# Hybrid recurrent block on one core: the first norm's token tiles transposed by products with a diagonal of their roots, norm weights as a scale of the operands, first units by column halves

## The chip, the core and the metric

The kernel runs on one core of a Trainium2 chip. The metric is the device time of one execution in microseconds (us); lower is better. The engines of the core are named as the profile names them: PE (TensorE, matrix products) with its weight loads PEld, DVE (VectorE), ACT (ScalarE), POOL (GpSimd) and SP (SyncE, which here only starts transfers). Data lie in SBUF, products land in PSUM banks.

## The reference

One layer over 528 tokens: 16 meta tokens ahead of 512 tokens of x, each of 1024 features. What the change touches is the first norm and the first columns of the product behind it.

```python
def rms_norm(x, g):
    y = x32 * lax.rsqrt(jnp.mean(x32 * x32, axis=-1, keepdims=True) + EPS)
    return (y * g.astype(jnp.float32)).astype(x.dtype)
...
    h = jnp.concatenate([meta, x], axis=1)
...
        xn = rms_norm(h, norm_mix_g[l])
        z = xn @ w_in[l]
        u_rnn, u_gate, q, k, v, g_ret, ga, gb = jnp.split(z, IN_SPLITS, axis=-1)

        xr = causal_dwconv(u_rnn, rnn_conv_w[l], rnn_conv_b[l])
        hr = rg_lru(xr, rg_a_w[l], rg_a_b[l], rg_x_w[l], rg_x_b[l], lru_lambda[l])
        o_a = hr * jax.nn.gelu(u_gate)
...
        mixed = (jax.nn.sigmoid(ga) * (o_a @ w_branch_rnn[l])
                 + jax.nn.sigmoid(gb) * (o_b @ w_branch_ret[l]))
        h = h + mixed @ w_out[l]
```

`u_rnn` has 1280 columns, ten blocks of 128; a gated linear recurrence runs on them (`rg_lru`, whose gates are two block-diagonal 128x128 products). Behind it come a retention branch with four heads, the mixture, a second norm, a convolved feed-forward part and a last norm. All are in f32, and the kernel keeps that accuracy.

## The kernel before, in words

**Operands in two parts.** Every f32 operand of a large product is split in two f16 parts: `split` (L90 to L92) writes the high part with ACT (L91: source times a scale, rounded to f16) and the rest with DVE (L92: source times scale minus high part). A product is then three f16 products, high by high, high by low and low by high (`project`, L370, and `project_half`, L383). The normed tokens lie transposed, feature on partition, in `xh` and `xl`: 8 feature blocks by 3 zeros and 528 tokens.

**Weights in units.** A unit is a block of weight columns. `unit_load` (L186) takes a raw f32 buffer out of a ring of two (`wraw`), starts its transfer, and gives back two steps that split the unit's two halves into `wt` tiles. The first ten blocks of `w_in` (the columns of `u_rnn`) are two units of 128 columns, one for each of blocks 0 and 1, and four units of 256 columns. Transfers are started on SP's queue in program order; `load` (L96) keeps them in that order. A transfer into a raw buffer starts when DVE has split what lay there.

**When steps are issued.** In the loops, `tick` takes the next split step of the queue unless the tiles from the unit in use up to that step's unit (two a unit) would be more than six; then it returns with nothing done. `get` issues what the next product needs. A step of unit u first starts the loads up to unit u+1.

**The prologue.** x comes in four token tiles of 128 tokens, two to a buffer `xin`. ACT squares and sums (L320), takes the root (L322), DVE inverts it (L324). `first_rows` (L398) multiplies the tile by its roots and by `gmix`, the norm weights broadcast to 128 partitions by a 512 KB transfer. `first_transpose` (L404) transposes its eight blocks on PE (L411), and `finish` splits them into `xh` and `xl`. The 16 meta tokens go another way: `xmeta` holds them as 128 rows of 128, a product with `same` (L442) sums their squares, and one with `pick` (L441) spreads the weights; then one transposition (L452). `keep_warm` (L424) is a number of products of zeros. `first_half(n)` (L388) multiplies block n of `u_rnn` with the first 267 columns, that is meta and tiles 0 and 1; `conv_product(n)` (L525) does the other half for n below 3, and whole blocks beyond. The order in the prologue, and in the whole kernel, is the order of the code: the engines run their instructions as written (`manual_schedule`, L429).

**The convolution loop** (L579 to L595) over n from 0 to 9: product n; at n of 0 the split of the gate weights "a" (`gw`); from n = 3 on, a tick and the gates of block n-3; then `conv_taps(n)`: ACT writes tap 3 with the bias (L537), DVE adds three taps (L539). For n below 2 a tick stands behind the taps. At n = 2 block 0 is split (`xs`, for the gates' product), then the gate weights "x", then block 1. The gates of block 0 run on PE between products 3 and 4 (L370 with `gw`), and their sigmoids on ACT (L556).

**Small vectors.** `v1`, `v2` hold convolution weights and biases row by row; after the last `first_half` three transpositions (L492 to L494) put them into PSUM as `ptv`, and DVE copies them out (L496 to L502: `vt1`, `vt2`, `gfT`, and `cwr`, the taps' factors).

`dec_meta`, a part of the decay table of the retention, is read from token chunk 0 of each head on (L718), and is loaded at L689.

## Time and profile before

| | |
|---|---|
| median of 3 runs | 1078.27 us (1078.19 to 1080.12) |
| profiled execution, its own time | 1080.82 us |
| its span | 1079.1 us |
| mean granted clock of PE | 0.998 |
| PE busy | 1059.0 us, 98% |
| DVE busy | 839.4 us, 78% |
| ACT busy | 568.2 us, 53% |
| POOL busy | 6.9 us, 1% |

A row of the timeline has the start in the span, the duration, the engine, the line, the operation, what it writes and reads, and shapes; "xN" is a run of N alike that stands as one row, its duration being from the first start to the last end. The brackets tell how long the engine had been idle, and what released it. In the chain of waits a row is start, duration, and what stood on the path that ended last. A row of the table of windows has the stretch and its length, then busy time and number of instructions for PE, PEld, DVE, ACT and POOL, the granted PE clock, the DMA engines' share and GB/s. DMA rows on SP are the issue alone; a reader's idle time shows the landing.

### The profile page before, as it was taken

What the parts mean: (1) busy time and instruction counts of PE and PEld (TensorE: products, weight loads), DVE (VectorE), ACT (ScalarE), POOL (GpSimd) and SP (SyncE); (2) the same over time, 40 slices, a digit from 0 to 9 for tenths busy, and PEclk for the clock granted to TensorE, in tenths of its full rate; (3) what the DMA queues carried; (4) which work ended last, traced back from release to release, by engine and by line L of the source; (5) the groups of instructions that cost most, each with busy time, mean ns of one, the idle gap of its engine ahead of it and who ended that gap; (6) DMA issues with size and microseconds to landing.
All of it is one profiled execution on the core that took longest, in us unless ns stands there. A gap on an engine that the chain in (4) does not pass through costs nothing.

```text
span 1079.1 us, 20969 instructions
## 1 busy us (share of the span) xinstructions
PE 1059.0 (98%) x9045; PEld 856.6 (79%) x9045; DVE 839.4 (78%) x1220; ACT 568.2 (53%) x847; POOL 6.9 (1%) x20
## 2 busy tenths in 40 slices
PE   8999999999999999999999999999999999999997
PEld 5888888875684858888888885588888888888885
DVE  5875699998786969888697785478767776888875
ACT  6568963534564747566454453364544454454442
POOL 2000000000000000000000000000000000000000
PEclk9999999999999999999999999999999999999999
DMA  6423243431211311433333355053232323113322
GB/s 209 143 92 104 79 138 118 157 119 40 75 45 50 108 64 65 125 91 118 104 103 118 118 199 173 2 196 115 81 118 80 118 79 118 40 60 121 115 79 79
DMA packets 105957, 112.02 MB, mean 104 GB/s; under 512 B 3470, under 2 KB 97396, under 8 KB 105864
## 3 DMA queue, kind: packets, MB, share of 16 engines
q1 hardware_dynamic: 105432, 110.27, 31.1%
q8 instruction: 71, 1.16, 0.4%
q10 hardware_dynamic: 144, 0.26, 0.1%
q14 instruction: 22, 0.18, 0.1%
q0 software_dynamic: 288, 0.14, 0.0%
HBM read 108.57 MB, written 2.10 MB: 103 GB/s over the span
## 4 chain that ended last, share of the span: by engine, by line
PE 71%; DVE 17%; ACT 8%; issue 2%; DMA 2%; SPq 0%; ACTq 0%; DVEq 0%
PE ps L370 33%; PE P L1247 9%; PE pa L775 7%; DVE wt L92 4%; PE ps L838 4%; PE pm L370 4%; PE ps L1119 3%; PE ps L383 3%; PE pe L775 3%; ACT wt L91 2%; PE pb L775 2%; PE ps L860 1%; DVE rnn L574 1%; DVE raw L231 1%; DMA raw<-in_w_out 1%
## 5 line engine op out<-in xcount | busy, mean ns | idle before, releaser
L370 PEld LDWEIGHTS <-wt 128*128 128x128 f16 x4224 | 410.5, 97 | 63.7 <-DVE t L666 1.4
L92 DVE SCALAR_TENSOR_TENSOR wt<-raw,wt 128x1024 f16<-128x1024 f32 (+2 forms) x270 | 296.2, 1110 | 71.7 <-ACT wt L91 69.8
L91 ACT ACTIVATE wt<-raw 128x1024 f16<-128x1024 f32 (+2 forms) x270 | 256.1, 964 | 161.3 <-PE ps L370 28.3
L775 PEld LDWEIGHTS <-wt 128*128 128x128 f16 x2016 | 195.0, 97 | 36.0 <-issue 8.8
L370 PE MATMUL ps<-x2h,wt 128*128 128x258 f16 x1440 | 218.8, 273 | 0.0
L370 PE MATMUL ps<-xh,wt 128*128 128x257 f16 (+2 forms) x1056 | 163.8, 275 | 1.1 <-DVE t L666 1.1
L370 PE MATMUL ps<-x2l,wt 128*128 128x258 f16 x720 | 137.7, 272 | 0.0
L1204 DVE SCALAR_TENSOR_TENSOR cv<-ps,vt,cv 128x512 f32<-128x512 f32 x96 | 71.9, 748 | 54.5 <-ACT cv L1202 53.2
L370 PE MATMUL ps<-xl,wt 128*128 128x257 f16 (+2 forms) x528 | 102.2, 275 | 0.0
L1247 PE MATMUL P<-wt,act 128*128 128x256 f16 x792 | 88.3, 273 | 0.0
L1247 PEld LDWEIGHTS <-act 128*128 128x128 f16 x792 | 77.5, 98 | 9.0
L838 PE MATMUL ps<-wt,xh 128*128 128x512 f16 x256 | 76.4, 379 | 1.2 <-DVE v L92 1.0
L775 PE MATMUL pa<-xs,wt 128*128 128x257 f16 x576 | 71.6, 273 | 4.8 <-ACT kept L780 4.5
L1202 ACT ACTIVATE cv<-ps,vt,vt 128x512 f32<-128x512 f32 x48 | 37.1, 774 | 56.8 <-PE ps L370 52.2
L370 PE MATMUL pm<-oa,wt 128*128 128x257 f16 x480 | 55.4, 274 | 0.0
L838 PEld LDWEIGHTS <-xh 128*128 128x128 f16 x256 | 24.8, 98 | 30.9 <-issue 2.9
L838 PE MATMUL ps<-wt,xl 128*128 128x512 f16 x128 | 48.5, 379 | 0.0
L775 PE MATMUL pa<-ob,wt 128*128 128x257 f16 x384 | 45.7, 274 | 0.6 <-ACT last L780 0.5
L1119 PE MATMUL ps<-wt,mx 128*128 128x512 f16 x192 | 44.8, 379 | 0.5 <-DVE mx L92 0.5
L231 DVE TENSOR_TENSOR raw<-raw 128x1024 f32<-128x1024 f32 x35 | 42.7, 1220 | 0.6
L1119 PEld LDWEIGHTS <-mx 128*128 128x128 f16 x192 | 17.4, 98 | 19.2 <-DVE mx L92 1.0
L860 PE MATMUL ps<-sc,v 128*128 128x257 f16 (+4 forms) x384 | 32.1, 236 | 0.0
(253 smaller groups left out, 1278.1 us busy)
## 6 DMA issues: line engine op xcount, KB each, us to landing
raw<-in_w_in SPq DMA_DIRECT2D x41, 1024.0 KB, 4.9
raw<-in_w_up SPq DMA_DIRECT2D x24, 1024.0 KB, 5.0
raw<-in_w_down SPq DMA_DIRECT2D x48, 256.0 KB, 3.6
raw<-in_w_branch_ret SPq DMA_DIRECT2D x16, 512.0 KB, 4.0
raw<-in_w_branch_rnn SPq DMA_DIRECT2D x8, 640.0 KB, 4.2
raw<-in_w_out SPq DMA_DIRECT2D x4, 1024.0 KB, 4.9
xin<-in_x SPq DMA_DIRECT2D x4, 512.0 KB, 6.6
h<-in_x SPq DMA_DIRECT2D x4, 512.0 KB, 4.9
```

Source lines behind the costliest of these rows:

```text
L91: nc.scalar.activation(hi, src, AF.Copy, scale=s)
L92: nc.vector.scalar_tensor_tensor(lo, src, s, hi, op0=ALU.mult, op1=ALU.subtract)
L231: nc.vector.tensor_tensor(pair, pair, rv[:, :, right].rearrange("p (h k) c -> p h k c", h=2), op=ALU.add)
L370: nc.tensor.matmul(ps[:, hf, :n], w(aw, k, col, P), src(ax, k, c0, n), start=k == 0 and (aw, ax) == (0, 0), stop=k == nk - 1 and aw == 1)
L383: nc.tensor.matmul(ps[:, hf, :n], w(aw, k, col, P), src(ax, k, c0, n), start=k == 0 and (aw, ax) == (0, 0), stop=k == KD - 1 and aw == 1)
L775: nc.tensor.matmul(ps[:, :257], ws[k // 4](wf, aw, k % 4), src(xf_, ax, k), start=first and k == 0 and (aw, ax) == (0, 0), stop=k == last_ ...
L838: nc.tensor.matmul(pb, xf(ax, k, XF + j0, nb), w(aw, k % 4, 0, 512), start=i == 0, stop=i == 23)
L860: nc.tensor.matmul(ps[:, hf, s0 - lo_i:257], vt[b][:, va, d * P:(d + 1) * P], st[SCP[b][0]][:, sa, o:o + hi_i - s0], start=i == 0, stop=i ...
L1119: nc.tensor.matmul(ps[:, n], mx[k][:, a, c0:c0 + P], wo[k // 2](aw, k % 2, n * 512, 512), start=j == 0, stop=j == 23)
L1202: nc.scalar.activation(vv_, ps[:, :, 2:258], AF.Identity, scale=vt2[:, 96 + ch:97 + ch], bias=b_ff[:, ch:ch + 1])
L1204: nc.vector.scalar_tensor_tensor(vv_, ps[:, :, j:j + 256], vt2[:, 48 * j + ch:48 * j + ch + 1], vv_, op0=ALU.mult, op1=ALU.add)
L1247: nc.tensor.matmul(pd[:, 256 * tt:256 * tt + 256], t[:, ax, c0 + tt * P:c0 + tt * P + P], w(wf, aw, i), start=q % 6 == 0 and tt == 0 and i ...
```

## The change

Each token tile was multiplied by its roots and the norm weights on DVE and then transposed. Now DVE makes a 128x128 diagonal of the tile's roots (`dg`), and PE multiplies each 128x128 block of the raw tile with that diagonal in f32; the product is the transposed block, already times the roots. The norm weight of a feature is now the weight of a partition, so it is applied as the scale operand when the product is split: `gs` holds eight columns of 128 weights, which PE transposes out of the 8x128 rows that `xmeta` already has. With one scale per block the split of a tile is eight ACT pieces and eight DVE pieces of 128x128 in place of two and two of 128x512. `gmix` and its transfer are gone. The transfer of the 8x128 weights moves from SP's queue to ACT's; that of `dec_meta` moves from the head of SP's queue into the chain of loads, behind a unit that is loaded much later.

The two units of 128 columns become one of 256, so that `u_rnn` is five units. The first two are loaded and split by column halves (`column_unit`): first the 128 columns of one block, then those of the other. Both are loaded in the prologue, so what was the third 256-column load there is gone. The products of zeros become 15, 4 and 6, from 18, 2, 5 and 6. The products of tiles 2 and 3 stand behind `first_half(1)` and behind `first_half(2)`; before, the transpositions stood behind `first_half(0)` and behind `first_half(1)`.

```diff
@@ -113,9 +113,7 @@
 
     o_ur, o_ug, o_q, o_k, o_v, o_gr, o_ga, o_gb = 0, 1280, 2560, 3584, 4608, 6656, 8704, 9728
     u_ur = []
-    for n in range(2):
-        u_ur.append((unit(8, P, [(0, 0, kmaj(w_in, 0, 8, o_ur + P * n, P))]), 0))
-    for i in range(1, 5):
+    for i in range(5):
         u = unit(8, 256, [(0, 0, kmaj(w_in, 0, 8, o_ur + 256 * i, 256))])
         u_ur += [(u, 0), (u, P)]
     u_ug = [unit(8, 256, [(0, 0, kmaj(w_in, 0, 8, o_ug + 256 * i, 256))]) for i in range(5)]
@@ -209,6 +207,30 @@
         wviews.append(lambda a, k, c0, m: tiles[k // hk][:, a, k % hk * ncol + c0:k % hk * ncol + c0 + m])
         return [step(i, c) for i in range(2) for c in range(cuts)]
 
+    def column_unit():
+        _, ncol, parts, _ = units[len(loaded)]
+        raw = wraw.tile([P, 2048], F32, name="raw")
+        rv = raw.rearrange("p (k c) -> p k c", c=ncol)
+        ap = parts[0][2]
+        tiles = []
+        def fetch(c):
+            load(rv[:, :, c * P:c * P + P], ap[:, :, c * P:c * P + P])
+        def step(i, c):
+            def run():
+                if c == 0:
+                    tiles.append(wsp.tile([P, 2, 1024], F16, name="wt"))
+                tv = [tiles[i][:, a].rearrange("p (k c) -> p k c", c=ncol)[:, :, c * P:c * P + P] for a in range(2)]
+                split(tv[0], tv[1], rv[:, 4 * i:4 * i + 4, c * P:c * P + P], SW)
+            return run
+        loaded.append(len(loaded))
+        wviews.append(lambda a, k, c0, m: tiles[k // 4][:, a, k % 4 * ncol + c0:k % 4 * ncol + c0 + m])
+        queue([step(i, c) for c in range(2) for i in range(2)])
+        return fetch
     def fast_steps(rv, bk, bc):
 
 
@@ -298,7 +320,6 @@
     nc.vector.memset(xh[:, :, 0:3], 0.0)
     nc.vector.memset(xl[:, :, 0:3], 0.0)
 
-    gmix = wsp.tile([P, D], F32, name="gmix", tag="wt")
     xmeta = work.tile([P, T], F32, name="xmeta", tag="w")
 
     same = work.tile([P, T], F32, name="same", tag="w")
@@ -343,16 +364,18 @@
     for i in range(2):
         xt = xslot([P, 2, D], F32, f"xin{i}")
         xin.append(xt)
+    nc.scalar.dma_start(xmeta[0:8, P:2 * P], norm_mix_g.rearrange("(c f) -> c f", f=P))
     load(xin[0][:, 0], x2[0:P])
     load(xin[0][:, 1], x2[P:2 * P])
-    load(gmix, norm_mix_g.partition_broadcast(P))
     load(xmeta[:, 0:P], meta.rearrange("t (c f) -> (t c) f", f=P))
-    load(xmeta[0:8, P:2 * P], norm_mix_g.rearrange("(c f) -> c f", f=P))
-    queue(unit_load())
+    fetch = column_unit()
+    fetch(0)
     load(xin[1][:, 0], x2[2 * P:3 * P])
-    queue(unit_load())
+    fetch(1)
     load(xin[1][:, 1], x2[3 * P:4 * P])
-    xn_t = {}
+    fetch = column_unit()
+    fetch(0)
+    fetch(1)
 
     SPLIT = ((0, 0), (0, 1), (1, 0))
 
@@ -395,27 +418,39 @@
     def token_rows(i):
         return xin[i // 2][:, i % 2]
 
-    def first_rows(i, rs):
-        xn_t[i] = pair("xn")
-        for a in range(2):
-            sl = slice(a * 512, (a + 1) * 512)
-            nc.vector.scalar_tensor_tensor(xn_t[i][a], token_rows(i)[:, sl], rs, gmix[:, sl], op0=ALU.mult, op1=ALU.mult)
-    def first_transpose(i, banks):
-        xn = xn_t.pop(i)
+    gs = const.tile([P, KD], F32, name="gs")
+    def first_scale(i):
+        rs = rms_scale(token_rows(i), P, "n")
+        dg = piece([P, 512], F32, "dg")[:, 0:P]
+        nc.vector.tensor_scalar_mul(dg, ident, rs)
+        return dg
+    def first_transpose(i, dg, banks):
         c0 = 3 + NM + P * i
-        pvs = []
-        for a in range(2):
-            pv = banks[a].rearrange("p (b c) -> p b c", c=P)
+        pvs = [b.rearrange("p (b c) -> p b c", c=P) for b in banks]
+        def turn(a):
             for k in range(4):
-                nc.tensor.transpose(pv[:, k], xn[a][:, k * P:(k + 1) * P], ident)
-            pvs.append(pv)
-        def finish(*half):
-            for a in half:
-                sl = slice(4 * a, 4 * a + 4)
-                split(xh[:, sl, c0:c0 + P], xl[:, sl, c0:c0 + P], pvs[a], S_XN)
-        return finish
+                c = 512 * a + k * P
+                nc.tensor.matmul(pvs[a][:, k], token_rows(i)[:, c:c + P], dg, start=True, stop=True)
+        def high(a):
+            for k in range(4):
+                g = gs[:, 4 * a + k:4 * a + k + 1]
+                nc.scalar.activation(xh[:, 4 * a + k, c0:c0 + P], pvs[a][:, k], AF.Copy, scale=g)
+        def low(a):
+            for k in range(4):
+                g = gs[:, 4 * a + k:4 * a + k + 1]
+                nc.vector.scalar_tensor_tensor(xl[:, 4 * a + k, c0:c0 + P], pvs[a][:, k], g,
+                                               xh[:, 4 * a + k, c0:c0 + P], op0=ALU.mult, op1=ALU.subtract)
+        return turn, high, low
 
     warm = work.tile([P, 512], F16, name="warm", tag="w")
     nc.vector.memset(warm, 0.0)
@@ -430,51 +465,68 @@
     def ptr_banks():
         return [bank("ptr") for _ in range(2)]
 
-    keep_warm(18)
-    pmeta = acc("pmeta")[:, 0]
-    xm, gm = xmeta[:, 0:P], xmeta[0:8, P:2 * P]
-    first_rows(0, rms_scale(token_rows(0), P, "n"))
-    finish0 = first_transpose(0, ptr_banks())
-    first_rows(1, rms_scale(token_rows(1), P, "n"))
-    ssm = small.tile([P, 4], F32, name="ssm")
-    nc.scalar.activation(xmeta[:, 2 * P:3 * P], xm, AF.Square, accum_out=ssm[:, 0:1])
-    nc.tensor.matmul(pmeta[:, 0:P], pick[0:8, 0:P], gm, start=True, stop=True)
-    nc.tensor.matmul(pmeta[:, 2 * P:2 * P + 1], same[:, 0:P], ssm[:, 0:1], start=True, stop=True)
-    finish0(0)
-    finish0(1)
-    keep_warm(2)
-    pt1 = acc("pt1")
-    finish1 = first_transpose(1, [pt1[:, 0], pt1[:, 1]])
-    nc.scalar.activation(ssm[:, 1:2], pmeta[:, 2 * P:2 * P + 1], AF.Sqrt, scale=1.0 / D, bias=eps_t)
-    nc.vector.reciprocal(ssm[:, 2:3], ssm[:, 1:2])
-    nc.vector.scalar_tensor_tensor(xm, xm, ssm[:, 2:3], pmeta[:, 0:P], op0=ALU.mult, op1=ALU.mult)
-    keep_warm(5)
-    nc.tensor.transpose(pmeta[:, P:2 * P], xm, ident)
-    keep_warm(6)
     def first_step():
         steps[done[0]][1]()
         done[0] += 1
 
+    keep_warm(15)
+    pmeta = acc("pmeta")[:, 0]
+    xm, gm = xmeta[:, 0:P], xmeta[0:8, P:2 * P]
+    ssm = small.tile([P, 4], F32, name="ssm")
+    dg0 = first_scale(0)
+    turn0, high0, low0 = first_transpose(0, dg0, ptr_banks())
+    turn0(0)
+    nc.tensor.transpose(pmeta[:, 3 * P:3 * P + 8], gm, ident[0:8, 0:8])
+    nc.vector.tensor_scalar_mul(gs, pmeta[:, 3 * P:3 * P + 8], S_XN)
+    turn0(1)
+    dg1 = first_scale(1)
+    pt1 = acc("pt1")
+    turn1, high1, low1 = first_transpose(1, dg1, [pt1[:, 0], pt1[:, 1]])
+    high0(0)
+    nc.scalar.activation(xmeta[:, 2 * P:3 * P], xm, AF.Square, accum_out=ssm[:, 0:1])
+    high0(1)
+    nc.tensor.matmul(pmeta[:, 0:P], pick[0:8, 0:P], gm, start=True, stop=True)
+    turn1(0)
+    nc.tensor.matmul(pmeta[:, 2 * P:2 * P + 1], same[:, 0:P], ssm[:, 0:1], start=True, stop=True)
+    turn1(1)
+    nc.scalar.activation(ssm[:, 1:2], pmeta[:, 2 * P:2 * P + 1], AF.Sqrt, scale=1.0 / D, bias=eps_t)
+    low0(0)
+    low0(1)
+    nc.vector.reciprocal(ssm[:, 2:3], ssm[:, 1:2])
+    nc.vector.scalar_tensor_tensor(xm, xm, ssm[:, 2:3], pmeta[:, 0:P], op0=ALU.mult, op1=ALU.mult)
+    keep_warm(4)
+    nc.tensor.transpose(pmeta[:, P:2 * P], xm, ident)
+    keep_warm(6)
     first_step()
-    finish1(0)
+    high1(0)
+    low1(0)
     split(xh[:, :, 3:3 + NM], xl[:, :, 3:3 + NM], pmeta[:, P:2 * P].rearrange("p (t c) -> p c t", c=8), S_XN)
     first_step()
-    finish1(1)
-    first_rows(2, rms_scale(token_rows(2), P, "n"))
+    high1(1)
+    low1(1)
     first_half(0)
-    for i in range(2):
-        first_step()
-    finish2 = first_transpose(2, ptr_banks())
-    rs3 = rms_scale(token_rows(3), P, "n")
-    finish2(0, 1)
-    first_rows(3, rs3)
+    first_step()
+    first_step()
+    dg2 = first_scale(2)
     first_half(1)
-    queue(unit_load(2))
-    for i in range(4):
-        first_step()
-    finish3 = first_transpose(3, ptr_banks())
+    turn2, high2, low2 = first_transpose(2, dg2, ptr_banks())
+    turn2(0)
+    turn2(1)
+    first_step()
+    first_step()
+    dg3 = first_scale(3)
+    for a in range(2):
+        high2(a)
+        low2(a)
     first_half(2)
-    finish3(0, 1)
+    turn3, high3, low3 = first_transpose(3, dg3, ptr_banks())
+    turn3(0)
+    turn3(1)
+    for a in range(2):
+        high3(a)
+        low3(a)
+    first_step()
+    first_step()
 
 
     v1 = work.tile([P, T], F32, name="v1", tag="w")
@@ -686,7 +738,7 @@
 
     dec = [piece([P, T], F32, f"dec{h}") for h in range(HEADS)]
     dec_meta = const.tile([P, HEADS, NM], F32, name="dec_meta")
-    nc.sync.dma_start(dec_meta, decay_t[:, :, T:].rearrange("h p c -> p h c"))
+    load(dec_meta, decay_t[:, :, T:].rearrange("h p c -> p h c"))
     for h in range(HEADS):
         nc.sync.dma_start(dec[h], decay_t[h, :, 0:T])
     sc = {}
```

SP's queue at the start of the program, before (`raw` are weight buffers, a number behind a name is one use of it):

```order
L689 DMA dec_meta_2836<-decay 128x4x16
L99 DMA xin0_110<-in_x 128x1024
L102 DMA xin0_110<-in_x 128x1024
L102 DMA gmix_99<-in_norm_mix_g 128x1024
L102 DMA xmeta_100<-in_meta_tokens 128x128
L102 DMA xmeta_100<-in_norm_mix_g 8x128
L102 DMA raw_117<-in_w_in 128x8x128
L102 DMA xin1_111<-in_x 128x1024
L102 DMA raw_120<-in_w_in 128x8x128
L102 DMA xin1_111<-in_x 128x1024
L102 DMA raw_316<-in_w_in 128x8x256
```

And after:

```order
L99 DMA xin0_109<-in_x 128x1024
L102 DMA xin0_109<-in_x 128x1024
L102 DMA xmeta_99<-in_meta_tokens 128x128
L102 DMA raw_115<-in_w_in 128x8x128
L102 DMA xin1_110<-in_x 128x1024
L102 DMA raw_115<-in_w_in 128x8x128
L102 DMA xin1_110<-in_x 128x1024
L102 DMA raw_120<-in_w_in 128x8x128 x2
L102 DMA raw_421<-in_rg_a_w 128x10x128
```

Three issues have left the head, and the first load into a buffer that has to be emptied is now the gates' (`raw_421`) instead of the unit `raw_316`.

PE around the last token tile, before (`ptr` and `ps` are PSUM banks, `xn` the normed tile):

```order
L383 LDWEIGHTS wt_263
L383 MATMUL ps_291<-xh_95,wt_263 128x267
L411 MATMUL ptr_328<-ident_86,xn0_287 128x128 x4
L411 MATMUL ptr_329<-ident_86,xn1_288 128x128 x4
L383 LDWEIGHTS wt_318
L383 MATMUL ps_338<-xh_95,wt_318 128x267
```

And after, where `wt_317` is the last of `first_half(2)` and `wt_218` the first of `conv_product(0)`:

```order
L406 LDWEIGHTS wt_317
L406 MATMUL ps_345<-xh_95,wt_317 128x267
L440 MATMUL ptr_370<-dg_327,xin1_110 128x128 x4
L440 MATMUL ptr_371<-dg_327,xin1_110 128x128 x4
L545 MATMUL ptv_411<-ident_86,v1_400 128x128
L546 MATMUL ptv_411<-ident_86,v2_401 128x128
L547 MATMUL ptv_411<-ident_86,v2_401 128x24
L406 LDWEIGHTS wt_218
L406 MATMUL ps_126<-xh_95,wt_218 128x267
```

Before, one first half stood between the last tile's transpositions and what follows; now its products stand directly ahead of `ptv` and the first `conv_product`.

ACT in the convolution loop, before (`rnn` is a block's convolution, `wt` the split of a unit, `xs` that of a block):

```order
L537 ACTIVATE rnn_428<-ps_125,vt1_93,cwr_386 128x528
L537 ACTIVATE rnn_459<-ps_291,vt1_93,cwr_386 128x528
L91 ACTIVATE wt_466<-raw_433 128x1024
L537 ACTIVATE rnn_493<-ps_338,vt1_93,cwr_386 128x528
L91 ACTIVATE xs_498<-rnn_428 128x528
```

And after:

```order
L589 ACTIVATE rnn_461<-ps_126,vt1_93,cwr_419 128x528
L91 ACTIVATE wt_470<-raw_466 128x1024
L589 ACTIVATE rnn_497<-ps_279,vt1_93,cwr_419 128x528
L91 ACTIVATE wt_502<-raw_466 128x1024
L589 ACTIVATE rnn_529<-ps_345,vt1_93,cwr_419 128x528
L91 ACTIVATE xs_534<-rnn_461 128x528
```

Since units 0 to 2 are now six tiles, the tick behind the taps of block 0 issues a step where it returned before; both splits of the next unit stand among the taps of blocks 0 to 2, ahead of the split of block 0, and the low parts on DVE stand in the same order.

## The prediction

> **What bounds the kernel now.** First the page's table of engines, then the chain of waits for the first 140 us:
>
> ```profile
> PE 1059.0 (98%) x9045; PEld 856.6 (79%) x9045; DVE 839.4 (78%) x1220; ACT 568.2 (53%) x847; POOL 6.9 (1%) x20
> ```
>
> ```profile
> 2.32 7.05 DMA gmix<-in_norm_mix_g
> 9.50 0.76 DVE xn L402
> ...
> 20.59 1.05 PE ptr L411 x8
> ...
> 28.68 8.37 PE ps L383 x72
> 37.05 47.73 PE ps L370 x414
> ```
>
> PE is the bound, so only two things matter: when its unbroken stream starts, and whether something makes it wait in the stream. The chain starts with the broadcast weights and is PE work from then on. The prologue decides the start; these are its rows in the timeline:
>
> ```profile
> 0.81 0.43 SPq L689 DMA_DIRECT2D dec_meta<-decay  x1
> 1.31 0.49 SPq L99 DMA_DIRECT2D xin<-in_x  x1
> 1.50 6.16 PE L426 MATMUL ps<-warm 128*128 128x512 f16 x18 [1.50 <-DVE warm L421]
> 5.18 1.06 ACT L320 ACTIVATE junk<-xin 128x1024 f16<-128x1024 f32 x1 [2.87 <-DMA xin<-in_x]
> 6.69 0.16 DVE L324 RECIPROCAL rs<-sd 128x1 f32<-128x1 f32 x1 [5.24 <-ACT sd L322]
> 9.50 1.41 DVE L402 SCALAR_TENSOR_TENSOR xn<-xin,rs,gmix 128x512 f32<-128x512 f32 x2 [2.65 <-DMA gmix<-in_norm_mix_g]
> 11.55 0.48 PE L441 MATMUL pmeta<-xmeta,pick 8*128 8x128 f32 x2
> 11.97 0.38 PE L442 MATMUL pmeta<-ssm,same 128*128 128x1 f32 x2
> 16.38 1.46 PE L426 MATMUL ps<-warm 128*128 128x512 f16 x6
> 17.68 0.28 PE L383 MATMUL ps<-xh,wt 128*128 128x267 f16 x1
> ```
>
> The roots are there at 6.85, but DVE waits 2.65 us for `gmix` until 9.50. PE has its first operand at 10.40 and starts `first_half(0)` at S = 17.68. In the table of windows PE stands empty in the first of these two and has about half its clock in the second:
>
> ```profile
> 7.70:10.30 2.60, 0.00 (x0) 0.00 (x0) 0.80 (x2) 0.69 (x3) 2.60 (x6) 1.00 1.07 347
> 12.40:16.20 3.80, 3.80 (x15) 2.51 (x14) 2.95 (x7) 1.37 (x3) 0.47 (x1) 0.55 0.51 191
> ```
>
> The convolution loop decides whether the stream is broken:
>
> ```profile
> 28.72 0.29 DVE L496 COPY vt<-ptv 128x128 f32<-128x128 f32 x1
> 29.30 1.62 DVE L92 SCALAR_TENSOR_TENSOR gw<-raw,gw 128x512 f16<-128x512 f32 x3
> 30.94 0.37 SPq L102 DMA_DIRECT2D raw<-in_w_in  x1
> 35.16 2.37 DVE L539 SCALAR_TENSOR_TENSOR rnn<-ps,cwr,rnn 128x528 f32<-128x528 f32 x3 [0.38 <-ACT rnn L537]
> 35.76 1.06 ACT L91 ACTIVATE wt<-raw 128x1024 f16<-128x1024 f32 x1 [0.64 <-DMA raw<-in_w_in]
> 37.45 1.21 DVE L92 SCALAR_TENSOR_TENSOR wt<-raw,wt 128x1024 f16<-128x1024 f32 x1
> 38.58 2.37 DVE L539 SCALAR_TENSOR_TENSOR rnn<-ps,cwr,rnn 128x528 f32<-128x528 f32 x3
> 40.86 0.70 DVE L92 SCALAR_TENSOR_TENSOR xs<-rnn,xs 128x528 f16<-128x528 f32 x1
> 42.45 1.51 PE L370 MATMUL ps<-xs,gw 128*128 128x264 f16 x12
> 42.59 1.28 ACT L556 ACT_TABLE_LOAD   x1
> 46.01 2.37 DVE L539 SCALAR_TENSOR_TENSOR rnn<-ps,cwr,rnn 128x528 f32<-128x528 f32 x3
> 50.71 0.39 PE L370 MATMUL ps<-xh,wt 128*128 128x267 f16 x2
> ```
>
> The gates of block 0 start on PE at 42.45, and DVE has their operand at 40.86 + .70 = 41.56: under 1 us of slack. Ahead of it the load issued at 30.94, when DVE had split the gate weights, lands at 35.76, 4.82 later, while DVE has the taps of block 1 (35.16) to do. `conv_product(5)` at 50.71 needs the bank that the taps of block 3 empty at 46.01 + 2.37 = 48.38: 2.3 us of slack.
>
> **The change part by part.** *The start.* Without `dec_meta` ahead of it the first x is issued .50 earlier (1.31 - .81), so the roots are ready at 6.35. The diagonal is one 128x128 DVE instruction; I take .29 from the copy at 28.72 and .1 between engines: 6.75. Three fewer products of zeros, .217 each (17.68 - 16.38 over six), let PE go at 7.66 - .65 = 7.01. So PE is free last, and nothing waits for `gmix`.
>
> *The price of the f32 products.* No row shows one of 128x128 by 128x128. A transposition of f32 leaves one record per instruction: eight in 1.05, .131 each. True products of f32 leave two: L441 and L442 have two records for one instruction, and so have these late rows of 257 columns, timed by the next start:
>
> ```profile
> 299.03 1.11 PE L875 MATMUL ps<-ssum,ones 128*128 128x257 f32 x4 [0.22 <-DVE ssum L868]
> 299.98 1.05 PE L775 MATMUL pe<-xs,wt 128*128 128x257 f16 x8
> ```
>
> Four records in .95 are .24 each, .12 for 128 columns: 16 records, 1.9 us a tile. By twice the transposition it is 2.10. I take 2.0, .95 more than before for each tile. The lower end is one record each, 1.05. The upper is the pair at L441 by the next start, 11.97 - 11.55 = .42 a product, 3.36 a tile, if weight loads do not overlap; nearest in shape are the rows of 128 rows, so the sum goes by 2.0. The Trainium skill, "FP8 and Floating Point Precision", section "TensorE Precision Notes", says true FP32 takes four passes through the array; at the f16 rate of the chain (47.73 over 414 products of about 267 columns, .115 each) that is an estimate of .22 a product and 1.76 a tile, by which the end would come about 1.0 earlier than the sum below. It lies between the ends taken from rows, and no run here yet separates it from the two records.
>
> *The new S.* 7.01, two tiles 4.0, the transposition of the weights .13, L441 .42, L442 .38, four products of zeros .87, the transposition of meta .11 (16.38 - 16.27, its start), six of zeros 1.30: 14.2, which is 3.5 before 17.68. DVE's last piece for `first_half(0)`, the low part of meta, is about there too (14.0). The splits in eight pieces:
>
> ```profile
> 16.58 0.28 ACT L91 ACTIVATE xh<-pmeta 128x128 f16<-128x128 f32 x1 [1.37 <-PE pmeta L452]
> 16.90 0.29 DVE L92 SCALAR_TENSOR_TENSOR xl<-pmeta,xh 128x128 f16<-128x128 f32 x1 [0.97 <-ACT xh L91]
> 20.79 1.28 DVE L92 SCALAR_TENSOR_TENSOR wt<-raw,wt 128x512 f16<-128x512 f32 x2
> ```
>
> A piece of 128x128 lasts .28 to .29, and I count .21 to .25 between starts; four are .85 to 1.0 against .64 for one of 128x512 (20.79, two in 1.28).
>
> *PE alone from there.* Tiles 2 and 3 add .95 each. The transpositions into `ptv`, now right behind tile 3, reuse the bank of tile 3's first half, so they wait for its low pieces on DVE. PE ends tile 3 at S + 3 x 2.75 + 2 x 2.0 = S + 12.25; its first half ends 1.0 before; four ACT pieces to S + 12.25, four DVE pieces to S + 13.2. PE waits .95. If PE had nothing else to wait for, the gates of block 0 would start at 42.45 - 3.5 + 1.9 + .95 = 41.8, a gain of .6. The rest of the 3.5 is gone.
>
> *DVE and the loads.* Behind S + 13.2 DVE has four more pieces (S + 14.05), the last two splits of unit 1 (1.2: S + 15.25), the copies out of `ptv` (29.30 - 28.72 = .58: S + 15.83) and the gate weights (1.62: S + 17.45 = 31.65). Only then may unit 2's load start: .7 later than its counterpart at 30.94. It lands 4.82 later, S + 22.3 = 36.5. In the new order the ACT split of this unit stands between the taps of blocks 0 and 1, and everything on ACT and DVE is queued behind it: 1.06 on ACT to S + 23.4; on DVE 1.13 (38.58 - 37.45) to 24.5, taps of block 1 2.29 to 26.8 (40.86 - 38.58 = 2.28 the like), the second split 1.13 to 27.95, taps of block 2 2.28 to 30.2, and the low part of block 0 .70 to S + 30.95 = 45.15. The gates start on PE two products (.23) before that operand is due, at 44.9: +2.5 against 42.45.
>
> *A second wait.* Unit 3's load goes into the buffer that the second split has emptied: S + 28.05, lands S + 32.9 = 47.1. ACT splits it ahead of the sigmoids of block 0: to 48.15. From the table load to the end of the taps of block 3 is 48.38 - 42.59 = 5.79: 53.95, and `conv_product(5)` starts at about 54.0, +3.3 against 50.71, though PE would be there at 53.2. Behind it PE has whole products between the gates and no row with so little slack, so +3.3 remains to the end.
>
> *No price.* `dec_meta` is used first at 240.0, and the issue (.43) lies in a queue whose loads take 4.9:
>
> ```profile
> raw<-in_w_in SPq DMA_DIRECT2D x41, 1024.0 KB, 4.9
> L718 DVE SCALAR_TENSOR_TENSOR sf<-ps,dec_meta x4: 161/163/164, 240.0 to 291.4; 128x16 f32<-128x16 f32 x4
> ```
>
> If it delayed a load that PE waits for, it would cost up to .9 (the issue and as much in transfer); I take 0. The 8x128 weights on ACT's queue are due at about 8.1; landing as late as x in the prologue (5.18 - 1.31 = 3.9 behind an issue near 2.3) they are in time, and 1 us late would be a cost of 1.
>
> **The sum.** +3.3 on the span, 1079.1 to 1082.4; the profiled execution's own time, 1080.82, would become 1084.1. It lies 2.55 above the median of 1078.27, so the median becomes 1081.6.
>
> **The rivals.** *The waits are covered.* If the load of unit 2 is issued or lands 3.4 us earlier than I have it (at S + 14.1 in place of 17.45), neither wait is on PE's path, and the gain of .6 stays: 1077.7, no change. For it speaks that the loop's load is only .7 later than before; against it that DVE has no gap in my count between S + 12.25 and S + 17.45. Chance .10; by one record a product besides, both waits, being tied to S, move 3.8 earlier, and without waits the end is 1073.9: faster, .07.
>
> *The products cost .42.* S moves by 2 x 1.36, and tile 2 and 3 push DVE by as much: 5.4 in all on top of 3.3 is 1087.0. For it: it is the only f32 product of this prologue. Against it: eight rows of contraction and the first in a group. Chance .11.
>
> *One record a product.* Then 3.8 go and the end is 1077.8: .03, since every product of f32 here that is no transposition has two.
>
> *The clock.* In 12.40:16.20 PE had .55 of its clock behind 2.60 without work. If such a stretch of 3.8 falls on the new prologue, it costs 1.9 and the end is 1083.5; it decides if PE stands for over about 2 us before S. For it: the first products of zeros are slow too (18 in 6.16, .34 against .217). Against it: my count has no gap there. The Trainium skill, "TensorE: Matmul & The Clock Gate", "Part 1: The HAM clock gate", puts such throttling behind an idle window of about 3.4 us, and its "Part 4: PE-mode transpose" says that transpositions do not count as busy; by both the products would hold the clock, which the slow stretch with its transpositions here fits. Chance .12.
>
> **How the numbers follow.** The main case, +1.8 to +5, has .57; .05 of it is within .2%, which is 2.16 us and about what a measurement of this kernel can tell from no change. Within: .10 + .03 + .05 = .18. Faster: .07. Slower: .52 + .11 + .12 = .75. The range goes from 1077.4, under the cases of no change, to 1087.0, the dear products; the main case's own is 1080.1 to 1083.3.
>
> **What would show it.** PE without a gap from 7.7 to 10.3, and 2.0 us for a tile's eight products; `first_half(0)` at 14.2; a wait of about .95 ahead of `ptv`; ACT idle for the first split in the loop until about 36.5, released by a transfer; PE waiting about 3 us for `xs` ahead of the gates of block 0, and under 1 us ahead of `conv_product(5)`. I am wrong if the load of unit 2 is issued well before 31, if a tile takes 3 us, or if PE waits further on.

## The result, and the profile after

The changed kernel takes 1088.68 us (median of 5, 1088.04 to 1089.33); the kernel before, run beside it, 1078.70 (1078.19 to 1080.40). The ratio is 1.0086, with a 95% interval of 1.0075 to 1.0098: slower by about 10 us, where 1081.6 was forecast and 1087.0 was the end of the range. The profiled execution has a span of 1087.6 against 1079.1.

The page's engines, after:

```profile
PE 1063.3 (98%) x9072; PEld 860.5 (79%) x9072; DVE 839.5 (77%) x1241; ACT 571.9 (53%) x871; POOL 6.9 (1%) x20
```

PE is busy 4.3 longer, a part of it at a lower clock, and the span is 8.5 longer, so about half of the loss is standing. The timeline of the prologue, after (L440 is the product with the diagonal, L406 the first halves and `conv_product`, L450 the low pieces):

```profile
6.41 0.29 DVE L428 TENSOR_SCALAR dg<-ident,rs 128x128 f32<-128x128 f32 x1
6.91 1.05 PE L440 MATMUL ptr<-dg,xin 128*128 128x128 f32 x8
...
14.06 0.28 PE L406 MATMUL ps<-xh,wt 128*128 128x267 f16 x1
...
19.80 1.95 PE L440 MATMUL ptr<-dg,xin 128*128 128x128 f32 x16
...
26.61 2.16 DVE L450 SCALAR_TENSOR_TENSOR xl<-ptr,gs,xh 128x128 f16<-128x128 f32 x8 [2.38 <-ACT xh L445]
27.79 0.33 PE L545 MATMUL ptv<-ident,v 128*128 128x128 f32 x1 [1.50 <-DVE xl L450]
```

The first half of block 0 starts at 14.06 (14.2 predicted); a tile's products cost 1.95 and leave two records each (2.0 predicted). The wait ahead of `ptv` is 1.50. The loop, after (L589 and L591 are the taps, L393 the whole products and the gates, L608 the sigmoids):

```profile
29.99 0.37 SPq L102 DMA_DIRECT2D raw<-in_rg_x_w  x1
32.11 27.67 SPq L102 DMA_DIRECT2D raw<-in_w_in  x4
39.02 1.06 ACT L91 ACTIVATE wt<-raw 128x1024 f16<-128x1024 f32 x1 [6.93 <-DMA raw<-in_w_in]
40.10 1.22 DVE L92 SCALAR_TENSOR_TENSOR wt<-raw,wt 128x1024 f16<-128x1024 f32 x1 [5.53 <-ACT wt L91]
42.96 0.38 PE L393 MATMUL ps<-xs,gw 128*128 128x264 f16 x2 [0.63 <-ACT xs L91]
46.95 0.70 DVE L92 SCALAR_TENSOR_TENSOR xs<-rnn,xs 128x528 f16<-128x528 f32 x1
47.70 2.36 PE L393 MATMUL ps<-xs,gw 128*128 128x264 f16 x10 [4.36 <-DVE xs L92]
49.75 1.06 ACT L91 ACTIVATE wt<-raw 128x1024 f16<-128x1024 f32 x1 [2.04 <-DMA raw<-in_w_in]
54.13 2.37 DVE L591 SCALAR_TENSOR_TENSOR rnn<-ps,cwr,rnn 128x528 f32<-128x528 f32 x3
```

The first issue at 32.11 is unit 2's, and its landing lets ACT go only at 39.02, 6.9 later. Until then DVE stands 5.53, and PE stands .63 and 4.36 ahead of the gates of block 0. Behind that wait ten products of the gates last 2.36 where twelve lasted 1.51 before. The table of windows shows why, in the granted clock (the figure behind the five engines):

```profile
47.70:53.40 5.70, 5.70 (x26) 3.82 (x26) 3.95 (x6) 3.63 (x6) 0.00 (x0) 0.50 0.79 264
53.40:57.00 3.60, 3.60 (x32) 2.98 (x30) 2.99 (x4) 1.16 (x3) 0.00 (x0) 0.96 0.03 9
```

The half clock begins while PE still stands and lasts 6.8, in 6.0 of which PE works:

```profile
43.46:46.87 3.41, 0.00 (x0) 0.00 (x0) 3.34 (x5) 1.33 (x3) 0.00 (x0) 1.00 0.29 77
46.87:53.69 6.82, 5.99 (x28) 4.01 (x28) 5.02 (x9) 4.55 (x6) 0.00 (x0) 0.50 0.80 269
```

Putting the same PE instruction of both traces side by side (counted from the end, where the programs are alike) gives the path of the loss; "block 5" is `conv_product(5)`:

| PE instruction | before | after | shift |
|---|---|---|---|
| first half of block 0 starts | 17.68 | 14.06 | -3.6 |
| first transposition into `ptv` | 28.13 | 27.79 | -0.3 |
| third product of the gates of block 0 | 42.67 | 47.70 | +5.0 |
| block 5 | 50.71 | 58.62 | +7.9 |
| branch stage, near 633 before | 632.68 | 640.93 | +8.3 |
| output stage, near 659 before | 659.19 | 667.77 | +8.6 |

The start's gain is gone by `ptv`, the wait at the gates costs 5.4, the slow clock 2.9, and .7 comes in two small steps late in the program, whose cause was not followed.

### The profile page after: what moved, and what is told of

It reads as the page before. It is cut to its first block, busy times and chain, and to the rows that moved or that the text cites. A ratio compares the mean times of both kernels' runs of the same rounds, so it can differ in the third digit from the quotient of the medians.

```text
span 1087.6 us, 21069 instructions
## 1 busy us (share of the span) xinstructions
PE 1063.3 (98%) x9072; PEld 860.5 (79%) x9072; DVE 839.5 (77%) x1241; ACT 571.9 (53%) x871; POOL 6.9 (1%) x20
## 4 chain that ended last, share of the span: by engine, by line
PE 72%; DVE 16%; ACT 8%; issue 2%; DMA 1%; ACTq 0%; DVEq 0%
PE ps L393 32%; PE P L1299 9%; PE pa L827 8%; PE ps L890 4%; PE pm L393 4%; DVE wt L92 4%; PE pe L827 3%; PE ps L1171 3%; ACT wt L91 2%; PE pb L827 2%; PE ps L406 2%; PE ps L912 1%; DVE rnn L626 1%; DVE raw L253 1%; ACT L678 1%
## 5 line engine op out<-in xcount | busy, mean ns | idle before, releaser
L393 PEld LDWEIGHTS <-wt 128*128 128x128 f16 x4224 | 411.5, 97 | 64.8 <-DVE t L718 1.4
L393 PE MATMUL ps<-x2h,wt 128*128 128x258 f16 x1440 | 218.8, 273 | 0.0
L393 PE MATMUL ps<-xh,wt 128*128 128x257 f16 (+2 forms) x1056 | 165.3, 277 | 1.1 <-DVE t L718 1.1
L393 PE MATMUL ps<-x2l,wt 128*128 128x258 f16 x720 | 137.8, 273 | 0.0
L393 PE MATMUL ps<-xl,wt 128*128 128x257 f16 (+2 forms) x528 | 103.0, 277 | 0.0
L393 PE MATMUL pm<-oa,wt 128*128 128x257 f16 x480 | 55.4, 274 | 0.0
```

The costliest lines, as they stand in the source:

```text
L393: nc.tensor.matmul(ps[:, hf, :n], w(aw, k, col, P), src(ax, k, c0, n), start=k == 0 and (aw, ax) == (0, 0), stop=k == nk - 1 and aw == 1)
```

## The experiments

The start of the first half of block 0 turned out to differ between executions of one kernel, so each profiled execution is also told by its own time less that start, that is what lies behind the prologue. In the first four rows, three kernels that have the program of before behind the prologue, it is the same within .4.

| profiled execution | start of first half | own time | difference |
|---|---|---|---|
| before | 17.68 | 1080.82 | 1063.1 |
| before, dec_meta moved (e7) | 14.24 | 1077.71 | 1063.5 |
| the same, timed (e9) | 14.76 | 1078.10 | 1063.3 |
| before, 24 products of zeros (e10) | 16.67 | 1079.97 | 1063.3 |
| before, with the new split order (e5) | 15.10 | 1080.71 | 1065.6 |
| changed | 14.06 | 1089.33 | 1075.3 |
| changed, dec_meta at the head (e11) | 14.69 | 1088.74 | 1074.0 |
| changed, loads swapped (e1) | 14.32 | 1083.84 | 1069.5 |
| changed, PE kept busy in its wait (e2) | 14.01 | 1090.30 | 1076.3 |
| changed, split order of before (e3) | 14.10 | 1083.91 | 1069.8 |
| changed, both splits late (e4) | 14.18 | 1086.12 | 1071.9 |
| changed, unit 1 split early (e6) | 13.73 | 1086.07 | 1072.3 |
| changed, four edits (e8) | 13.79 | 1080.20 | 1066.4 |

**The clock (e2).** PE gets work in its wait:

```diff
             ps = acc("ps")
+            if n == 0 and nm == "a":
+                for _ in range(22):
+                    nc.tensor.matmul(ps[:, 0], xh[:, 0, 3:131], xh[:, 0, 3:515], start=True, stop=True)
```

> The changed kernel, with 22 products whose result is overwritten (512 columns of xh, .217 each, 4.8 in all) on PE right ahead of the gates of block 0, that is in its wait. Theory A (a wait of about 5 also costs the clock: products run at about half rate from 47.7 to 53.4, worth 2.9): the operand still comes at 47.65, but the products behind it run at full rate; the shift against the kernel before stays at +5.0 and the span is about 1084.7. Theory B (the slow products come from something else at that time, such as the transfers that run from 46 to 55 at 200 GB/s): the products stay slow and the span stays at 1087.6.

The timeline of this kernel (L607 are the added products), then one window:

```profile
42.11 4.93 PE L607 MATMUL ps<-xh 128*128 128x512 f16 x22
48.32 1.28 PE L393 MATMUL ps<-xs,gw 128*128 128x264 f16 x10 [1.05 <-DVE xs L92]
57.28 0.40 PE L393 MATMUL ps<-xh,wt 128*128 128x267 f16 x2 [0.77 <-DVE rnn L591]
```

```profile
48.30:52.00 3.70, 3.68 (x33) 3.12 (x33) 3.17 (x6) 1.53 (x3) 0.00 (x0) 1.00 0.70 209
```

The operand came .6 later still (48.3), but ten products of the gates lasted 1.28, under transfers of 209 GB/s at that time. So the slow products are the clock and not the transfers: theory A. Behind it PE now waits .77 at block 5, the second wait that the prediction had; in the changed kernel PE was so late that it was not seen. Block 5 starts at 57.28 in place of 58.62. The median did not show it (1089.15, ratio 1.0091, interval 1.0067 to 1.0114), and the expected span of 1084.7 was missed (1088.6): in the profiled execution another 3.0 come in the branch and output stages, 2.3 more than in the changed kernel, since loads landed late there (ACT stands 5.6 for the load of `w_out`, 3.6 in the changed kernel). Whether the other executions lost it in the same place is not known.

**The load that lands late (e1).**

```diff
     load_gates("a")
+    queue(unit_load())
     load_gates("x")
```

> The changed kernel, with the load of the unit for blocks 4 and 5 issued ahead of the load of the gate weights x. In the changed kernel it is issued at 32.11 behind that load (29.99) and its split begins only at 39.02, 6.9 later. Theory A (the late landing, because two loads share the DMA engines, makes PE wait for the split of block 0 and with it the slow clock): the load now goes at 29.99 and lands 4.9 later, at 34.9; the operand of the gates of block 0 is there at 43.6 in place of 47.65, PE waits about 1 at 42.3 and under 1 at the product of block 5, and keeps its clock; span about 1081.5 against 1087.6. Theory B (the place of the splits among the taps alone makes the wait, the landing is no matter): the wait stays near 5 and the span near 1087.

```profile
30.25 0.37 SPq L102 DMA_DIRECT2D raw<-in_w_in  x1
35.55 1.06 ACT L91 ACTIVATE wt<-raw 128x1024 f16<-128x1024 f32 x1 [3.21 <-DMA raw<-in_w_in]
44.24 1.29 PE L393 MATMUL ps<-xs,gw 128*128 128x264 f16 x10 [1.42 <-DVE xs L92]
```

The unit is there 5.3 after its issue, PE waits 1.42 with its clock kept, and .6 at block 5. Median 1083.54, ratio 1.0038 (1.0023 to 1.0053), span 1082.1: theory A, .6 off. The landing decides the size of the wait.

**The order of the splits (e3, e4, and e5 from the other side).**

```diff
-        if n < 2:
+        if n == 1:
             tick()
```

> The changed kernel, without the split step behind the taps of block 0: the order of splits and taps is the one of the kernel before (one step behind the taps of block 1, the next ahead of the gates of block 0). Theory A (order and landing together make the wait): the taps of block 1 no longer wait for the landing at 39.0, only those of block 2 do; these end at 43.6, the operand of the gates is there at 44.3, PE waits about 1.8 and keeps its clock, nothing waits at block 5; span about 1081.3. Theory B (the prologue alone is late, the order is no matter): the wait stays near 5 and the span near 1087.

```profile
40.09 1.06 ACT L91 ACTIVATE wt<-raw 128x1024 f16<-128x1024 f32 x1 [5.21 <-DMA raw<-in_w_in]
45.36 1.28 PE L393 MATMUL ps<-xs,gw 128*128 128x264 f16 x10 [2.56 <-DVE xs L92]
```

In this execution the unit landed at 40.1, 8.0 behind its issue at 32.14, a full us later than in the changed kernel; still PE waited only 2.56, kept its clock and waited nowhere else. Median 1083.34, ratio 1.0037 (1.0024 to 1.0050), span 1082.2 where 1081.3 was expected. Theory A holds: by the order of before, the taps of block 1 do not stand behind the landing.

```diff
-        if n < 2:
-            tick()
         if n == 2:
             conv_split(0)
+            tick(2)
```

> The changed kernel, with both split steps moved from behind the taps of blocks 0 and 1 to behind the split of block 0. Theory A (two separate waits, as predicted): the gates of block 0 no longer wait (operand at 40.0, PE there at 42.3). But the next unit's load goes only when the second split is done, about 42.5, lands at 47.4, and its split stands ahead of the sigmoids: the taps of block 3 end at 54.2, so PE waits at the product of block 5 from 50.6 to 54.3, 3.7: span about 1082.7 if the clock holds through 3.7 of idling, up to 1085.6 if it drops. Theory B (only the first wait matters, nothing is late behind it): span 1079, as the kernel before.

The timeline's row of ACT, then the table of PE's waits:

```profile
48.75 1.06 ACT L91 ACTIVATE wt<-raw 128x1024 f16<-128x1024 f32 x1 [4.57 <-DMA raw<-in_w_in]
```

```profile
PE ps L393 <- DVE rnn L591: 2.2, 1, 2.2
PE ps L393 <- ACT rnn L608: 2.0, 1, 2.0
```

The wait at the gates of block 0 is gone, and the second one has come in full: the next unit's split stands ahead of the sigmoids and starts at 48.75, and PE waits 2.0 for a bank of the sigmoids and 2.2 for the taps. The clock held. Median 1086.65, ratio 1.0067 (1.0052 to 1.0082). The span is 1084.4, and with the clock held 1082.7 was expected: there are two waits of 4.2 together and one of .3 at the gates of block 0 where one of 3.7 was expected, and .5 more comes in the late stages. So the split order has two prices, as predicted, and moving both steps exchanges one for the other.

The order alone, in the kernel before:

```diff
+        if n == 0:
+            ahead[0] = 8
         if n < 2:
             tick()
+        ahead[0] = 6
```

> The kernel before, with the order of splits among the taps that the change brings, and nothing else: a split step also behind the taps of block 0, so both splits of the unit for blocks 4 and 5 stand ahead of the split of block 0. Theory A (this order is enough to make PE wait, and the landing only sets how long): the load lands at 35.76 as before, its split now stands ahead of the taps of block 1, the operand of the gates of block 0 is there at 44.4 in place of 41.56 and PE waits 1.7 at 42.4; the next unit's load goes at 41.5 and its split ahead of the sigmoids ends near 47.5, so the product of block 5 starts at 53.3 against 50.71; span 1081.7. Theory B (the order costs nothing without the changed prologue): span 1079.1.

```profile
8.61 1.41 DVE L402 SCALAR_TENSOR_TENSOR xn<-xin,rs,gmix 128x512 f32<-128x512 f32 x2 [1.68 <-DMA gmix<-in_norm_mix_g]
33.09 1.06 ACT L91 ACTIVATE wt<-raw 128x1024 f16<-128x1024 f32 x1 [3.29 <-DMA raw<-in_w_in]
41.78 1.28 PE L370 MATMUL ps<-xs,gw 128*128 128x264 f16 x10 [1.50 <-DVE xs L92]
```

Median 1080.87 beside 1078.94, ratio 1.0015 (1.0006 to 1.0024). PE waits 1.50 at the gates of block 0 and .5 at block 5: the mechanism as expected. The span is 1079.0 and not 1081.7, since this execution started its first half at 15.10 and not at 17.68. Behind the start it is 1065.6 against 1063.1 to 1063.5, so 2.1 to 2.5 for the order alone, where 2.6 was expected. The start of before is taken up below.

**Why the load lands late (e6).**

```diff
+    first_step()
+    first_step()
     for a in range(2):
         high3(a)
         low3(a)
-    first_step()
-    first_step()
```

> The changed kernel, with the last two split steps of the second unit moved ahead of the splits of token tile 3, into time in which DVE and ACT have nothing to do (24.2 to 26.6 on DVE). Theory A (the load lands late because that raw buffer comes free only at 29.95, so the gate weights x go at 29.99 and share the DMA engines with the unit behind them): the gate weights x go at about 25.6 and land by 31, the unit goes at about 30.8, 1.28 earlier, and lands 4.9 to 5.3 later, near 36; the operand of the gates of block 0 is there at 44.4, PE waits 1.8 with its clock kept, and the product of block 5 starts at 53 to 53.4; span 1081.7 to 1082. Theory B (6.9 from issue to landing is the price of this load at this place whoever shares the engines): it lands at 37.7, the wait is 3.4 and the span 1084 or more.

```profile
25.13 0.37 SPq L102 DMA_DIRECT2D raw<-in_rg_x_w  x1
...
30.58 27.35 SPq L102 DMA_DIRECT2D raw<-in_w_in  x4
37.04 1.06 ACT L91 ACTIVATE wt<-raw 128x1024 f16<-128x1024 f32 x1 [5.28 <-DMA raw<-in_w_in]
45.72 2.33 PE L393 MATMUL ps<-xs,gw 128*128 128x264 f16 x10 [3.50 <-DVE xs L92]
```

The gate weights x went 5 us earlier, and the unit at 30.58, but ACT could split it only at 37.04, 6.5 later (5.3 by theory A, 6.9 by B): nearer theory B. PE waited 3.50 and then had half its clock:

```profile
45.70:49.20 3.50, 3.48 (x17) 2.39 (x17) 2.97 (x6) 1.32 (x3) 0.00 (x0) 0.51 0.65 197
```

Median 1085.91, ratio 1.0056 (1.0042 to 1.0070). So a load sharing the DMA engines is not the whole cause. The view of the DMA queues for 31 to 35 us, and then for 35 to 36.6, has this:

```profile
q8 instruction: 1, 0.02, 1.9%
```

```profile
DMA packets 39, 0.04 MB, mean 22 GB/s; under 512 B 4, under 2 KB 39, under 8 KB 39
```

One packet of instruction code took 1.9% of sixteen engines over 4 us, 1.2 us of one engine, and the last 39 packets then came at 22 GB/s, the rate of about one engine, when the rest of the load was done. Such a packet stands near this load in all thirteen traces. In six (changed, e2, e3, e4, e6, e11) it begins 1.3 to 2.3 behind the load's issue, and the load takes 6.5 to 8.0; in the other seven it begins 4.2 behind the issue or later, and the load takes 4.7 to 5.3. In five of the six the gate weights x also go 2.1 ahead of it; e6 alone has the packet without them. That the packet held the load back is read from this, not shown by a run of its own: in the changed kernel the end of the load, 37 to 38.6, moves 99 GB/s, so more than one engine was late there, and with the gate weights x 2.1 ahead the load took 6.8 to 8.0, so both may count. The Trainium skill, "DMA: Bandwidth & Descriptors", section "Queues, rings and completion order", says that one copy is split over up to 16 engines' rings and that each engine consumes its ring in order; the late tail agrees with that.

**The start (e7, e9, e10, e11).** The first is the move of `dec_meta` alone, in the kernel before:

```diff
-    nc.sync.dma_start(dec_meta, decay_t[:, :, T:].rearrange("h p c -> p h c"))
+    load(dec_meta, decay_t[:, :, T:].rearrange("h p c -> p h c"))
```

> The kernel before, with the dec_meta transfer moved from the head of SP's queue into the chain of loads, as the change does, and nothing else. By the prediction: the first transfer of x goes .50 earlier, gmix too, and the first half of block 0 starts near 17.2 in place of 17.68; span 1078.6. Rival: gmix lands when the DMA engines are done with all the bytes ahead of it, and the start stays at 17.7; span 1079.1.

It gave a first half at 14.24 in one execution, 3.4 earlier than the profile of before and almost the changed kernel's start, with DVE starting on gmix at 7.75; neither of the two answers. A timed series followed:

> The kernel before with dec_meta in the chain of loads and nothing else, now timed. In one execution its first half of block 0 started at 14.24 (against 17.68 in the profile of before, and 14.06 in the changed kernel), since gmix landed at 7.75 in place of 9.50 and PE, with 0.2 of idling, kept its clock. Theory A (PE is the bound behind that point and nothing else moved): every execution is like that one, median 1077.0 to 1078.0, that is .5 to 1.3 under the faster executions of before (1078.2 to 1078.7) and 2 to 3 under its slower ones. Theory B (that one execution was a lucky landing): median as before, in the same two groups.

```profile
8.27 1.41 DVE L402 SCALAR_TENSOR_TENSOR xn<-xin,rs,gmix 128x512 f32<-128x512 f32 x2 [2.03 <-DMA gmix<-in_norm_mix_g]
9.16 1.23 PE L411 MATMUL ptr<-ident,xn 128*128 128x128 f32 x8 [1.53 <-DVE xn L402]
14.76 0.28 PE L383 MATMUL ps<-xh,wt 128*128 128x267 f16 x1
```

Median 1078.55 beside 1078.61, ratio .9999 (.9990 to 1.0008): theory B. Six executions lie between 1077.9 and 1078.6, five between 1079.0 and 1080.1. The issue is worth too little to be seen in the median, whose interval leaves room for about 1 us. The kernel before falls in two groups more clearly: of 55 executions beside these experiments 34 lie between 1078.0 and 1079.3 and 21 from 1079.9 up. Its profile, 1080.82, is one of the upper ones, and it has a stretch at .55 of the clock from 12.4 to 16.2. Next, more products of zeros:

```diff
-    keep_warm(18)
+    keep_warm(24)
```

> The kernel before with 24 in place of 18 products of zeros at the start, and nothing else. Theory A (the executions of before fall in two groups, 1078.2 to 1078.7 and 1080.0 to 1080.8, because in some PE stands for 2.7 ahead of the first transpositions and then runs 3.8 at about half its clock, worth 1.9 to 2.5; the profile of before shows one of the slower): PE now stands under 1.5, no stretch at half clock, and all executions are in one group near 1078.5. Theory B (the groups come from the DMA landings alone): two groups as before.

```profile
9.40 1.23 PE L411 MATMUL ptr<-ident,xn 128*128 128x128 f32 x8 [1.17 <-DVE xn L402]
16.67 0.28 PE L383 MATMUL ps<-xh,wt 128*128 128x267 f16 x1
```

```profile
12.40:16.20 3.80, 3.80 (x18) 2.48 (x17) 2.24 (x6) 1.23 (x3) 0.51 (x1) 0.72 0.46 177
11.15:14.56 3.41, 3.41 (x14) 2.44 (x15) 2.51 (x6) 1.40 (x4) 0.51 (x1) 0.50 0.94 324
```

Median 1078.47, ratio 1.0000 (.9992 to 1.0009), seven executions at 1078.3 to 1078.6 and four at 1080.0 to 1080.2: still two groups, so that idling of 2.7 is their cause fell. The link between the group and the clock did not: the profile of this kernel, of the upper group, has the slow stretch after a wait of only 1.17, while e9, of the lower group, waited 1.53 and kept its clock. From the first transposition to the first half of block 0 it takes 5.60 in e7 and e9 and 5.59 in e5, all at full clock, and 7.28 in before and 7.27 in e10, both with half clock for 3.41 of it. These 1.7 are also the distance of the two groups of e10. The difference column is 1063.3 in e9 and e10. Last, the changed kernel with `dec_meta` at the head again:

> The changed kernel with the dec_meta transfer put back at the head of SP's queue. If the first transfer's place is worth what it is in the changed prologue by its rows: x lands .5 later, the roots are ready at 6.8, PE starts the products at 7.2 and the first half of block 0 at 14.4 to 14.6 against 14.06; all behind it is up to .5 later; span 1087.6 to 1088.1. So the products and the missing gmix transfer alone bring the start from 15.1 (before, with the clock kept) to about 14.5.

```profile
14.69 0.28 PE L406 MATMUL ps<-xh,wt 128*128 128x267 f16 x1
```

First half at 14.69, span 1087.0, one execution at 1088.74: the start a little later than the expected 14.4 to 14.6, the end within what executions differ. Against a start of 15.1 with the clock kept (e5), the products with the diagonal and the missing gmix bring .4, and the order of SP's queue another .6. These are estimates from single executions: with the changed prologue as it is the start lies between 13.73 and 14.32 in seven of them.

**All mended (e8).** Four edits of the changed kernel: the early split steps of e6, the swapped loads of e1, the order of e3, and the three transpositions into `ptv` with their copies moved between the first halves of blocks 0 and 1.

> The changed kernel with four edits: the last two split steps of the second unit ahead of the splits of token tile 3; the three transpositions of small vectors and the copies behind them between the first halves of blocks 0 and 1 instead of behind tile 3; the load of the unit for blocks 4 and 5 ahead of the gate weights x; no split step behind the taps of block 0. Theory A (the waits behind the prologue, and not the products with the diagonal, ate the earlier start): PE has no wait of 1.5 ahead of the small transpositions, the unit lands near 31, nothing waits at the gates of block 0 or at block 5, and PE is about 1.4 ahead of the kernel before from 41 on; span 1077.2 to 1078. Theory B (the products and the pieces of 128x128 cost what the start gained, so no mending of waits helps): span 1079 or more.

The table of PE's waits, of the rows up to block 5 the only one, and the timeline's row of the gates of block 0:

```profile
PE ps L406 <- DVE xl L450: 0.6, 1, 0.6
```

```profile
40.95 1.51 PE L393 MATMUL ps<-xs,gw 128*128 128x264 f16 x12
```

No wait at the gates or at block 5, and PE is there 1.5 ahead of the profile of before. Median 1080.38 beside 1078.94, ratio 1.0010 (1.0001 to 1.0018). The waits are gone but for .6, as theory A said; the span, 1078.4, lies between the two theories (up to 1078, from 1079), and the median is above that of before. So without the waits the change still brings nothing. Behind the start it is 1066.4 against 1063.3: two tiles' products .9 each, a wait of .6 for the low pieces of tile 3, and small steps in the late stages. The 1.3 by which it starts earlier than the 15.1 of e5 is less than that. The four edits were run together, so what each is worth here is not shown. No kernel timed here beats the one before by more than its interval.

## Why the prediction was wrong

- **The way and the places were right.** Start at 14.06 (14.2), 1.95 for a tile (2.0), a load behind DVE's splits, its split ahead of the taps of block 1, and PE waiting there for block 0's operand; e3 and e5 show that this order is the mechanism, e4 that the second wait exists.
- **"lands 4.82 later, S + 22.3 = 36.5".** It was issued at 32.11 (31.65 predicted) and there at 39.02. From there to the operand's end it took 8.63, and 8.65 was predicted. So the landing was mis-sized by 2.1 and DVE's chain by .5. I took the duration of one load in the trace of before, although the change issues the gate weights x at 29.99, 2.1 ahead of it, where they went at 27.20 before; e1 shows what the place is worth, e6 that this is not all.
- **The clock rival stood in the wrong place.** I asked for it only ahead of S ("it decides if PE stands for over about 2 us before S") and left the wait that I predicted myself, in the loop, without a price. It cost 2.9: half clock from 46.9 to 53.7. e2 shows that this is the clock. The bound of about 2 us is not borne out either: half clock came behind a wait of 1.17 in e10, and not behind one of 2.56 in e3. In the prologue the clock held as I argued (full from 5.9 to 46.9 in the changed kernel). The price that I gave such a stretch, 1.9, is too high by its own row: .45 of 3.8 is 1.7, and 1.7 is what the prologues of before and e10 lost. In the loop it cost more, because half clock lasted twice as long.
- **"the conv_product(5) starts at about 54.0, +3.3".** +7.9: +5.0 at the gates, +2.9 of the clock, and no second wait left over (.8 in the prediction), since PE was later than the taps.
- **"It lies 2.55 above the median".** I carried this over as a constant. It belonged to the prologue of that one execution: its start, 17.68, is 2.6 behind the 15.1 of e5, 1.7 by the slow stretch (the window 12.40:16.20 stood in my own rows) and .9 since DVE could start on gmix only at 9.50 and not at 8.61. The median points the same way: 1078.27 less the 1063.3 behind the start is 15.0. Against a start of about 15.1 the changed start gains 1, not 3.5, so by the same chain the median would have been 1081.6 + 2.5 = 1084.1 even with the loads as I had them.
- **The ends.** 1084.1, 2.5 more at the gates, 2.9 of the clock, .8 less for the second wait and .7 of the late stages make 1089.4, which is the profiled execution's time (1089.33); the median is .65 below it, where 2.55 had been taken off, and that is the last 1.9 of the 7.1 by which the forecast missed. The range's upper end came from dear products (.42), which did not occur, so it held none of the three causes.
- **Small terms.** The wait ahead of `ptv` was 1.50 for .95: ACT's first piece began 1.1 behind the start of tile 3's products, DVE's 1.2 behind ACT's, and DVE's four pieces took 1.2 (1.0, 1.0 and .95 in the prediction). `dec_meta` at 0 in its new place is borne out by e9 (1063.3 behind the start, 1063.1 before).

## What to carry to other kernels

Before a duration of a load is moved to another place, look at what the queue ahead of it now holds there; a wait of PE that is predicted to be several us needs a second price, that of the clock behind it. When the profiled execution lies 2 us off the median, find the rows that make it so before any gain is counted against it. And a prologue's gain has to be followed through every wait behind it: here 3.6 us were spent by the next 14 us of program.

## What the runs showed of the hardware

- The clock's drop has no sharp bound in the length of the wait: half clock came behind waits of PE of 1.17 (e10), 2.73 (before), 3.50 (e6), .56 plus 4.34 (e11) and .63 plus 4.36 (changed), and not behind 1.42 (e1), 1.53 (e9), two of about 2.1 close together (e4) and 2.56 (e3). It came in steps of one length: half clock lasted 3.41 in before, e6 and e10, and 6.83, twice that, in changed and e11. The price was about half of PE's work inside it: 2.9 of 5.99 in changed, 1.7 of 3.41 in e6. In the 3.41 ahead of the drop PE worked 0 (changed), .07 (e6), 1.40 (e11), 2.22 (before) and 2.25 (e10); in before and e10 1.2 of that are transpositions, and whether these count less than products no run isolates. So the length of the wait alone does not tell whether the clock drops; where it falls against these steps may decide, which is not shown. The Trainium skill, "TensorE: Matmul & The Clock Gate", "Part 1: The HAM clock gate", says that the window is free-running, about 3.4 long, and that a kernel's slow products vary from run to run with it; the steps of 3.41 and the two groups of executions of one kernel agree with that, while the drop behind 1.17 lies below the idle window of about 3.4 that it states.
- A 1 MB load of the same weights took 4.7 to 8.0 us from issue to the reader's start within these kernels, and an f32 product of 128x128 by 128 columns .24 (eight in 1.95), in two records of .12.
